# TensorE in recorded order, and memory given out by the recorder's clock, in a two-layer hybrid encoder trunk

## The chip, the core and the metric

The kernel runs on one core of one Trainium2 chip. The metric is the time of one execution on the device in microseconds; the median of several runs is taken. The engines are named as in the profile: PE is TensorE, DVE is VectorE, ACT is ScalarE, POOL is GpSimd, SP issues most DMAs.

## The reference

Two layers over a sequence of 256 tokens with 2048 channels. Each layer normalises, projects once to the columns of four token mixers and of four merge gates, runs the mixers, projects each mixer's output back, merges, and applies an output projection:

```
h = rms_norm(x, norm_g)
proj = h @ w_in                      # 13*512 + 256 + 4*2048 columns
A: ya = a_bg * conv3(a_cg * a_x) * silu(a_z)
B: yb = gqa_attention(rope(q), rope(k), v) * silu(b_z)
C: yc = rwkv7_bidir(h, c_r, c_k, c_v, ...) * silu(c_z)   # a scan in each direction
D: yd = silu(layer_norm(conv31(d_val * sigmoid(d_gate)) + dw_b)) * silu(d_z)
merged = sum_k sigmoid(gate_k + b_gate_k) * (y_k @ w_branch_k)
x = x + merged @ w_out
```

After both layers one more RMSNorm is applied. All is float32.

## The kernel before

Activations lie transposed: channels on the 128 partitions, the 256 tokens along the free axis. **The main stream** is the projections. Their weights arrive in 612 chunks of 128x1024 (`raw`), prefetched by DMA. `fetch` splits each chunk into two parts that TensorE takes at its fast rate: `hi`, a rounded copy made by ACT, and `lo`, the rest, made by DVE. `chunk` keeps three of them ahead. `wide` multiplies a chunk: for each of 8 blocks of 128 columns one `hi` matmul of 512 columns (x's own hi and lo side by side), and then for each block one `lo` matmul of 256 columns. `tile_b` makes one output tile of two chunks in a PSUM buffer `mg` (3 of them); `tile_branch` projects a mixer's output in the one buffer `mb`. After a tile `whole` adds its two halves: an ACT copy and a DVE addition, `arena<-mg`.

**The side work** is the four mixers: small float32 matmuls into four PSUM buffers `sd`, with ACT and DVE work between any two that hang together. In the trace and below, `bdS`, `bdT`, `bdE`, `bdM`, `bdR`, `bdX` and `rd` are constant buffers of mixer C, `part` is a two-part operand of A, B and C's norms. Mixer C's `rwkv` builds for each direction the inverses of small triangular blocks (`inverses`: two rounds of 32x32 products, `bdX` and then `bdT`, with an ACT copy each) and then goes through chunks of 64 tokens in sequence, two at a time (`chunks`). Mixer D's `conv_d` is 31 multiply-adds on DVE per 128 channels, all reading one input `u` and handed out three at a time; the tile `u` is given back at the end.

**Two things set the order.** First, the recorder: while `wide` and `passes` write down the projections, they call `pump` after each matmul, and `pump` steps the mixers, which are Python generators, where the kernel's own clock says that they are due. `now` is that clock's TensorE time; `clk` holds the times up to which DVE and ACT are taken; `due` is when the work of the step under way should be done. A step is next taken `SLACK` = 0.4 us after its `due`, and only while no engine of `clk` is further ahead of `now` than the side stream's `lead` (1.7 us and more). Second, the framework's scheduler goes over everything recorded after `first_x` and sets its own order on every engine, by priorities and its own estimates. Splits and prefetches are recorded at a high priority.

**The arena** is one SBUF tile from which the short-lived buffers of both streams come. `a` takes a piece (`Arena.get`), `f` gives it back (`Arena.put`) at recording time. Who gets the words next must wait on the engines for the last user. `get` prefers, among free stretches, those not given back within the last RECENT = 6 calls of `get` and `put`, then the tightest; pieces to keep (`keep`) come first-fit from the low end.

Of the kernel before, what the change touches and what calls it, by code (L numbers as in the profile page):

```python
# [21 lines left out]
DEPTH = 2  # L22
# [80 lines left out]
class Arena:  # L103


    U = 32
    RECENT = 6

    def __init__(self, ap, words):
        self.ap, self.n = ap, words // self.U  # L110
        self.when = np.zeros(self.n, np.int64)
        self.used = np.zeros(self.n, bool)
        self.live = {}
        self.tick = 0
        self.peak = 0

    def get(self, words, keep=False, take=True):

        m = -(-words // self.U)
        self.tick += 1  # L120
        best = None
        i = 0
        while i < self.n:
            if self.used[i]:
                i += 1
                continue
            e = i
            while e < self.n and not self.used[e]:
                e += 1
            if e - i >= m:  # L130

                j = i if keep else e - m
                key = i if keep else (int(self.when[j:e].max()) > self.tick - self.RECENT, e - i - m, -i)
                if best is None or key < best[0]:
                    best = (key, j)
            i = e
        if best is None:
            if not take:
                return False
            raise MemoryError(f"arena: {words} words asked, {(~self.used).sum() * self.U} free, live "  # L140
                              + str(sorted((v[1] * self.U, v[2]) for v in self.live.values())))
        j = best[1]
        if not take:
            return True
        self.used[j:j + m] = True
        self.peak = max(self.peak, int(self.used.sum()) * self.U * 4)
        return j, m
# [1 line left out]
    def free(self):  # L149
        return int((~self.used).sum()) * self.U  # L150

    def put(self, j, m):
        self.tick += 1
        self.used[j:j + m] = False
        self.when[j:j + m] = self.tick


class Side:
# [6 lines left out]
class Engine:  # L165
# [5 lines left out]
    def __getattr__(self, op):  # L171
        f = getattr(self.real, op)

        def call(out, *args, **kw):
            k = self.k
            if op == "preload_act_table_set":
                k.clk["scalar"] = max(k.clk["scalar"], k.now) + 1.3
                return f(out)  # L178
# [12 lines left out]
            else:  # L191
# [10 lines left out]
                else:  # L202
                    k.due = max(k.due, k.now) + cost
            return f(out, *args, **kw)  # L204

        return call
# [8 lines left out]
class Kern:  # L215
# [3 lines left out]
    RAW = 8  # L219
    BUSY = 0.7  # L220
    SLACK = 0.4
    LEAD = 1.7
    TWAIT = 24.0
    XSTEP = 1.0
# [30 lines left out]
    def a(self, shape, keep=False):  # L255
        words = int(np.prod(shape[1:]))
        if self.cur is None:

            t = self.now
            while not self.arena.get(words, keep, False) and self.now < t + 50:  # L260
                self.now += 0.2
                self.pump()
        j, m = self.arena.get(words, keep)
        if self.cur:
            self.cur.purse.net += m * Arena.U
        ap = self.arena.ap[:, j * Arena.U:j * Arena.U + words]
        if len(shape) > 2:
            names = "abcd"[:len(shape) - 1]
            ap = ap.rearrange(f"p ({' '.join(names)}) -> p {' '.join(names)}",
                              **{k: v for k, v in zip(names, shape[1:])})  # L270
        self.arena.live[id(ap)] = (ap, m, str(shape), j)
        return ap
# [9 lines left out]
    def f(self, *aps):  # L282
        for ap in aps:
            _, m, _, j = self.arena.live.pop(id(ap))
            self.arena.put(j, m)
            if self.cur:
                self.cur.purse.net -= m * Arena.U

# [24 lines left out]
    def add(self, gen, lead=None):  # L313

        e = Side(gen, self.now, lead or self.LEAD)
        if self.cur:
# [13 lines left out]
    def step(self, e):  # L330
# [9 lines left out]
        else:  # L340
            e.at = self.now + c if c > 0 else e.due + self.SLACK

# [386 lines left out]
    def conv_d(self, acc, i, u):  # L729
        nc = self.nc  # L730
        w = lambda j: self.pc("dw_w", j * NT + i)
        a = acc[:, i]
        nc.vector.tensor_scalar(a, u[:, 0:S], w(0), self.dwb2[:, i:i + 1], ALU.mult, ALU.add)
        for j in range(1, 31):
            nc.vector.scalar_tensor_tensor(a, u[:, j:j + S], w(j), a, ALU.mult, ALU.add)
            if j % 3 == 0:
                yield 0.9
        self.f(u)
# [48 lines left out]
    def rwkv(self, rkv, tl, cz):  # L787
# [5 lines left out]
        for d in range(2):  # L793
# [160 lines left out]
            for p in range(NT):  # L954
# [7 lines left out]
                for half in range(2):  # L962
# [9 lines left out]
                    def mm2(lhs, rhs, c0=0):  # L972
                        ps = self.pside()
                        for c in range(c0, 2):
                            a, b = cols[c]
                            self.blocks(ps[:, a:b], lhs(c), rhs[:, a:b], True, True)
                        return ps
# [165 lines left out]
    def layer(self, l):  # L1143
# [11 lines left out]
        for o, n, w, f in ((self.w0h, "w0", 8, 0.5), (self.a0h, "a0", 8, 0.5), (self.kah, "k_a", 4, 0.5),  # L1155
                           (self.dwb2, "dw_b", 4, 2.0), (self.gnb2, "gn_b", 4, 2.0)):
            nc.vector.tensor_scalar(o, par(n, w), f, None, ALU.mult)
# [179 lines left out]
    def run(self):  # L1337
        self.src = self.stream()
        self.ready, self.raws = [], []
        self.tiles = 0  # L1340
        self.consts()
        self.first_x()
        for l in range(DEPTH):
            self.layer(l)


@with_exitstack
# [5 lines left out]
def constants():  # L1353
# [4 lines left out]

    i = np.arange(P)
    put("ident", np.eye(P))  # L1360
    put("bdones", (i[:, None] // 64 == i[None, :] // 64) * 1.0)
    put("ones", np.ones((P, P)))

    perm = np.zeros((P, P))
# [105 lines left out]
```

## Time and profile before

| | us |
|---|---|
| median of 3 runs (1992.22 to 1999.15) | 1995.13 |
| the profiled execution | 1995.8 |
| its span on the core | 1993.9 |
| TensorE busy | 1934.8 |
| VectorE busy | 1439.8 |
| ScalarE busy | 1268.9 |

TensorE is busy through nearly all of the span. The rows that this text leans on stand in a section of their own below; a busy TensorE includes time in which its clock is granted at half, so both columns, busy and clock, have to be read.

### The profile page before, as it was taken

Reading aid. Unit: us, or ns where it says so; the run is one execution under the profiler, and the core shown is the slowest. Engines: PE = TensorE matmul, PEld = TensorE weight load, DVE = VectorE, ACT = ScalarE, POOL = GpSimd, SP = SyncE. Lnnn points to the kernel's source line nnn. Section 1 sums busy time; section 2 is a strip of 40 time slices with the busy share of each in tenths; the row PEclk is TensorE's granted clock in tenths of the full one; section 3 lists DMA queues with packets and bytes.
Section 4 is the critical chain, followed back from the end, with each engine's and each line's share of the span. In section 5 each row is a group of like instructions: output and inputs, shape, how many; then the busy total and the mean of one; then the engine's idle time right before and its main releaser. Section 6 shows DMA issues by size and latency. Waiting matters only on the chain.

```text
span 1993.9 us, 32440 instructions
## 1 busy us (share of the span) xinstructions
PE 1934.8 (97%) x12194; PEld 1716.7 (86%) x12194; DVE 1439.8 (72%) x2495; ACT 1268.9 (64%) x2293; POOL 71.6 (4%) x117
## 2 busy tenths in 40 slices
PE   8999999899999999999999999998999999999997
PEld 6888788799988898998888887888999989989986
DVE  7867858967787566666677778589787866566655
ACT  6776666567657766554567766766774577565454
POOL 1001010000101000000000010000001100000000
PEclk9999999899999999999999999999999999999998
DMA  7554443344655345566655554533555544456653
GB/s 247 186 181 165 159 156 117 117 165 166 197 181 180 137 150 179 202 206 205 214 186 185 181 169 143 154 114 138 177 171 187 195 143 159 155 184 207 203 190 136
DMA packets 97693, 343.19 MB, mean 172 GB/s; under 512 B 11808, under 2 KB 12192, under 8 KB 97536
## 3 DMA queue, kind: packets, MB, share of 16 engines
q1 hardware_dynamic: 93312, 331.48, 49.1%
q0 software_dynamic: 3648, 8.59, 1.7%
q8 instruction: 96, 1.57, 0.3%
q10 hardware_dynamic: 576, 1.05, 0.1%
q14 instruction: 61, 0.50, 0.1%
HBM read 332.48 MB, written 8.39 MB: 171 GB/s over the span
## 4 chain that ended last, share of the span: by engine, by line
PE 93%; ACT 3%; DVE 2%; DMA 1%; issue 1%; DVEq 0%; SPq 0%; POOL 0%; ACTq 0%; POOLq 0%
PE mg L204 74%; PE sd L204 9%; PE mb L204 9%; DVE arena L204 1%; DVE lo L204 1%; ACT arena L204 1%; ACT bdE L204 1%; DMA raw<-w 1%; ACT hi L204 1%; DMA scratch<-arena 0%; DMA arena<-xT 0%; ACT bdS L204 0%; ACT L178 0%; ACT bdT L204 0%; ACT bdR L204 0%
## 5 line engine op out<-in xcount | busy, mean ns | idle before, releaser
L204 PE MATMUL mg<-slab,hi 128*128 128x512 f32 x4368 | 1113.7, 396 | 17.1 <-DVE slab L204 9.5
L204 DVE TENSOR_TENSOR lo<-raw,hi 128x1024 fp32r<-128x1024 f32 x612 | 746.6, 1221 | 344.1 <-PE mg L204 247.2
L204 PEld LDWEIGHTS mg<-slab,hi 128*128 128x128 f32 x4368 | 789.6, 190 | 160.9 <-DVE slab L204 10.7
L204 ACT ACTIVATE hi<-raw 128x1024 fp32r<-128x1024 f32 x612 | 646.4, 1057 | 440.4 <-PE mg L204 294.7
L204 PE MATMUL mg<-slab,lo 128*128 128x256 f32 x4368 | 618.4, 285 | 1.7 <-DVE lo L204 1.5
L204 PEld LDWEIGHTS mg<-slab,lo 128*128 128x128 f32 x4368 | 585.9, 191 | 37.5 <-DVE lo L204 3.0
L204 DVE TENSOR_TENSOR arena<-arena 128x512 f32<-128x512 f32 (+16 forms) x389 | 166.1, 432 | 35.2 <-ACT arena L204 24.2
L204 DVE SCALAR_TENSOR_TENSOR arena<-arena,par 128x256 f32<-128x256 f32 x346 | 152.2, 479 | 7.8 <-ACT arena L204 6.7
L204 PE MATMUL mb<-slab,hi 128*128 128x256 f32 (+1 forms) x1040 | 156.8, 288 | 1.0 <-DVE slab L204 0.6
L204 PEld LDWEIGHTS mb<-slab,hi 128*128 128x128 f32 x1040 | 141.1, 192 | 5.7 <-DVE slab L204 0.8
L204 DVE TENSOR_TENSOR arena<-mg,arena 128x256 f32<-128x256 f32 x305 | 126.8, 418 | 18.0 <-ACT arena L204 15.3
L204 ACT ACTIVATE arena<-mg 128x256 f32<-128x256 f32 x241 | 89.7, 377 | 67.4 <-PE mg L204 52.3
L204 ACT ACTIVATE arena<-arena 128x256 f32<-128x256 f32 (+4 forms) x195 | 93.5, 497 | 29.5 <-DVE arena L204 26.1
L204 ACT ACTIVATE arena<-arena,b_gate 128x256 f32<-128x256 f32 x128 | 64.0, 503 | 54.9 <-DVE arena L204 54.4
L204 PE MATMUL mb<-slab,lo 128*128 128x256 f32 x528 | 87.2, 286 | 0.0
L178 ACT ACT_TABLE_LOAD x62 | 79.5, 1283 | 8.3 <-PE sd L204 5.0
L204 PEld LDWEIGHTS mb<-slab,lo 128*128 128x128 f32 x528 | 75.1, 192 | 1.6
L204 ACT ACTIVATE bdE<-sd 64x128 f32<-64x128 f32 x256 | 69.7, 272 | 7.5 <-PE sd L204 4.2
L204 DVE SCALAR_TENSOR_TENSOR slab<-arena,slab 128x512 fp32r<-128x512 f32 (+1 forms) x64 | 35.4, 555 | 34.8 <-ACT slab L204 34.7
L204 ACT ACTIVATE arena<-sd 128x64 f32<-128x64 f32 (+4 forms) x122 | 40.0, 332 | 17.3 <-PE sd L204 15.5
L204 DVE SCALAR_TENSOR_TENSOR arena<-arena 128x256 f32<-128x256 f32 (+1 forms) x80 | 37.1, 473 | 17.6 <-ACT arena L204 16.9
L204 PE MATMUL sd<-arena,bdE 128*128 128x128 f32 (+1 forms) x224 | 45.4, 285 | 3.9 <-ACT arena L204 3.3
(96 smaller groups left out, 1062.2 us busy)
## 6 DMA issues: line engine op xcount, KB each, us to landing
raw<-w SPq DMA_DIRECT2D x612, 512.0 KB, 3.3
arena<-xT SPq DMA_DIRECT2D x4, 512.0 KB, 8.3
scratch<-slab POOLq DMA_DIRECT2D x16, 128.0 KB, 2.7
scratch<-arena POOLq DMA_DIRECT2D x8, 256.0 KB, 4.2
arena<-xT SPq DMA_DIRECT2D x8, 256.0 KB, 3.8
x<-arena SPq DMA_DIRECT2D x8, 256.0 KB, 4.8
arena<-x SPq DMA_DIRECT2D x8, 256.0 KB, 3.6
arena<-lorab POOLq DMA_DIRECT2D x16, 96.0 KB, 2.9
```

The lines of the kernel that those rows point to most:

```text
L178: return f(out)
L204: return f(out, *args, **kw)
```

## The change

```diff
 class Arena:
     U = 32
-    RECENT = 6
...
-        self.when = np.zeros(self.n, np.int64)
+        self.when = np.zeros(self.n)
...
-    def get(self, words, keep=False, take=True):
+    def get(self, words, keep=False, take=True, now=0.0):
...
-                key = i if keep else (int(self.when[j:e].max()) > self.tick - self.RECENT, e - i - m, -i)
+                late = self.when[j:j + m].max() > now
+                key = (late, j) if keep else (late, e - i - m, -i)
...
-    def put(self, j, m):
-        self.tick += 1
+    def put(self, j, m, when):
         self.used[j:j + m] = False
-        self.when[j:j + m] = self.tick
+        self.when[j:j + m] = when
...
 class Kern:
     SLACK = 0.4
+    OVER = 1.5
...
-        j, m = self.arena.get(words, keep)
+        j, m = self.arena.get(words, keep, now=self.now)
...
-            self.arena.put(j, m)
+            self.arena.put(j, m, max(self.now, self.due, *self.clk.values()) + self.OVER)
...
-        for l in range(DEPTH):
-            self.layer(l)
+
+        with self.tc.manual_schedule(engines={mybir.EngineType.PE}):
+            for l in range(DEPTH):
+                self.layer(l)
```

In the two layers TensorE's instructions stay in the order in which they were recorded; ACT, DVE, POOL and SP are still ordered by the scheduler. A freed piece is stamped with the clock's latest time plus 1.5 us, and a request takes pieces whose stamp has passed by `now` before others. What is recorded is the same in both kernels: the same instructions in the same sequence (the numbers in the names differ by 2). In before TensorE's order steps back in the recorded sequence at 472 places, in after at one. The TensorE instructions that carry a wait go from 179 to 119, those of ACT from 839 to 749, those of DVE from 729 to 741.

**Place 1, DVE, mixer C's first direction in layer 0.** `arena<-sd_466,rd` makes the operand of the next `sd` matmul of the chunk sequence; the `par0` rows are `conv_d`, the `lo` rows are weight splits. Before:

```order
L204 SCALAR_TENSOR_TENSOR arena_69<-arena_69,par0_71 128x256 [waits DVE_49] x6
L204 TENSOR_TENSOR lo_524_3902<-raw_514_3842,hi_523_3901 128x1024 [waits DMAHW5_49,PE_49,Activation_49]
L204 SCALAR_TENSOR_TENSOR arena_69<-arena_69,par0_71 128x256 [waits DVE_49] x6
L204 TENSOR_TENSOR lo_529_3947<-raw_522_3899,hi_528_3946 128x1024 [waits DMAHW6_49,PE_49,Activation_49]
L204 TENSOR_TENSOR arena_69<-sd_466_3478,rd_105 128x64 [waits DVE_49]
L204 TENSOR_TENSOR arena_69<-sd_466_3478,consts_70 128x64
L204 SCALAR_TENSOR_TENSOR arena_69<-arena_69,par0_71 128x256 [waits DVE_49] x12
```

After:

```order
L202 TENSOR_TENSOR lo_461_3440<-raw_455_3404,hi_460_3439 128x1024 [waits DMAHW2_49,PE_49]
L202 TENSOR_SCALAR arena_69<-arena_69,par0_71,derived0_189 128x256 [waits DVE_49]
L202 SCALAR_TENSOR_TENSOR arena_69<-arena_69,par0_71 128x256 [waits DVE_49]
L202 TENSOR_TENSOR arena_69<-sd_466_3480,rd_105 128x64 [waits PE_49]
L202 TENSOR_TENSOR arena_69<-sd_466_3480,consts_70 128x64
L202 MEMSET arena_69 128x15 [waits DVE_49]
```

The operand stood behind runs of six `conv_d` rows and waited for DVE (for the last reader of its arena words, a `conv_d` row); now it stands some 30 rows earlier in DVE's queue, behind the split `lo_461` in place of `lo_529`, and waits for TensorE's product alone.

**Place 2, some 40 us further on, ACT, DVE and TensorE.** ACT's `arena<-sd_507` copies what the matmul `sd_512` takes (in before `sd_512` is `sd_512_3819` and reads the same copy). ACT before:

```order
L204 ACTIVATE arena_69<-mg_498_3732 128x256 [waits DVE_49]
L204 ACTIVATE arena_69<-mg_508_3804 128x256
L204 ACTIVATE arena_69<-sd_502_3751,arena_69 128x128 [waits PE_49]
L204 ACTIVATE arena_69<-sd_507_3790 128x256 [waits PE_49]
L204 ACTIVATE arena_69<-arena_69,b_gate0_188 128x256 [waits DVE_49] x2
```

ACT after:

```order
L202 ACTIVATE hi_510_3809<-raw_503_3767 128x1024 [waits DVE_49,DMAHW3_49,PE_49,Activation_49]
L202 ACTIVATE arena_69<-mg_498_3734 128x256 [waits DVE_49,PE_49]
L202 ACTIVATE hi_515_3846<-raw_509_3807 128x1024 [waits DVE_49,DMAHW4_49,PE_49,Activation_49]
L202 ACTIVATE arena_69<-arena_69,b_gate0_190 128x256 [waits DVE_49]
L202 ACTIVATE arena_69<-sd_507_3792 128x256 [waits DVE_49]
```

DVE after:

```order
L202 TENSOR_TENSOR lo_505_3770<-raw_499_3735,hi_504_3769 128x1024 [waits DMAHW2_49,PE_49,Activation_49]
L202 SCALAR_TENSOR_TENSOR arena_69<-arena_69,par0_71 128x256 [waits DVE_49]
L202 TENSOR_TENSOR arena_69<-mg_498_3734,arena_69 128x256 [waits Activation_49]
L202 SCALAR_TENSOR_TENSOR arena_69<-arena_69,par0_71 128x256 [waits DVE_49] x20
L202 TENSOR_TENSOR arena_69<-sd_512_3821,rd_105 128x64 [waits PE_49]
```

TensorE after (`sd_3792` is `sd_507`, `sd_3821` is `sd_512`):

```order
L202 MATMUL sd_3792<-bdE_83,bdT_77 128x128 x2
L202 MATMUL mg_3734<-slab_210,lo_3671 128x256 x4
L202 MATMUL mg_3806<-slab_207,hi_3737 128x512 x4
L202 MATMUL mg_3806<-slab_208,hi_3737 128x512 x4
L202 MATMUL sd_3821<-arena,bdE_83 128x128
```

The copy waited for its product alone; now it waits for DVE, and by the count in the built program that is the fifteenth of the twenty `conv_d` rows in one run, which stand behind the addition of tile `mg_498`. On TensorE four `lo` and eight `hi` matmuls lie between the product and the matmul that takes the copy. The same rows stand in layer 1 around `sd_1845`.

**Place 3, TensorE, the inverses of layer 0's second direction.** `sd_6191` (`sd_6193` after) is the `bdT` round of 32 products; ACT copies its result twice (32x512 each) before `sd_6227` (`sd_6229`) may start. Before:

```order
L204 MATMUL sd_6191<-bdT_77,arena 32x32
L204 MATMUL mg_6412<-slab_205,lo_6343 128x256 x2
L204 MATMUL sd_6191<-bdT_77,arena 32x32 x31
L204 MATMUL mg_6412<-slab_205,lo_6343 128x256 x2
L204 MATMUL mg_6412<-slab_206,lo_6343 128x256 x4
L204 MATMUL mg_6412<-slab_207,hi_6376 128x512 x4
L204 MATMUL mg_6412<-slab_208,hi_6376 128x512 x4
L204 MATMUL mg_6412<-slab_207,lo_6377 128x256 x4
L204 MATMUL mg_6412<-slab_208,lo_6377 128x256 x4
L204 MATMUL sd_6227<-bdE_83,bdT_77 128x128 x2
L204 MATMUL sd_6257<-arena,bdE_83 128x128
```

After:

```order
L202 MATMUL mg_6122<-slab_209,hi_6092 128x512 x4
L202 MATMUL mg_6122<-slab_210,hi_6092 128x512 x3
L202 MATMUL sd_6193<-bdT_77,arena 32x32 x32
L202 MATMUL mg_6122<-slab_210,hi_6092 128x512
L202 MATMUL sd_6229<-bdE_83,bdT_77 128x128 x2
L202 MATMUL mg_6122<-slab_209,lo_6093 128x256 x4
```

Twenty-two matmuls of projections recorded later lay between the two steps; now one `hi` matmul does. The same rows stand at four places, one for each direction and layer.

## Rows read from the trace of the kernel before

**Rows 1.** The page's head and busy times: engine, busy us (share of span), instructions.

```profile
span 1993.9 us, 32440 instructions
PE 1934.8 (97%) x12194; PEld 1716.7 (86%) x12194; DVE 1439.8 (72%) x2495; ACT 1268.9 (64%) x2293; POOL 71.6 (4%) x117
```

**Rows 2.** Busy times by stretch: start:end, length, busy (instructions) of each engine, clock, DMA.

```profile
200.00:250.00 50.00, 46.44 (x261) 38.70 (x261) 44.72 (x105) 31.76 (x60) 0.00 (x0) 1.00 0.47 158
...
300.00:350.00 50.00, 47.24 (x280) 42.48 (x281) 41.50 (x94) 33.28 (x86) 0.00 (x0) 0.93 0.36 121
350.00:400.00 50.00, 42.19 (x252) 37.51 (x251) 49.52 (x112) 28.91 (x64) 0.00 (x0) 0.90 0.32 112
...
700.00:1000.00 300.00, 300.00 (x1853) 269.91 (x1852) 189.35 (x259) 166.85 (x262) 0.00 (x0) 1.00 0.58 193
...
1350.00:1400.00 50.00, 46.14 (x290) 41.43 (x291) 48.59 (x103) 29.40 (x70) 0.00 (x0) 0.97 0.40 137
...
1981.00:1994.00 13.00, 0.04 (x1) 0.00 (x0) 5.83 (x6) 2.17 (x3) 3.43 (x2) 0.61 0.43 162
```

**Rows 3.** Chain of waits: start, length, what; its first and longest runs of matmuls.

```profile
9.46 20.28 PE mg L204 x96
...
908.92 88.83 PE mg L204 x507
```

**Rows 4.** TensorE's waits over the whole span: releaser, total us, times, longest.

```profile
PE sd L204 <- ACT bdS L204: 10.7, 8, 2.4
...
PE mg L204 <- DVE arena L204: 7.0, 4, 3.5
PE sd L204 <- ACT arena L204: 4.8, 10, 1.1
...
PE sd L204 <- ACT bdT L204: 2.2, 2, 1.3
```

**Rows 5.** Columns as in Rows 2, the six stretches at half clock.

```profile
1216.00:1222.70 6.70, 6.29 (x19) 5.13 (x19) 5.26 (x16) 1.44 (x2) 0.00 (x0) 0.50 0.10 39
...
sum 34.10, PE 31.59 PEld 28.17 DVE 27.02 ACT 12.87 POOL 0.00; mean PE 5.27 PEld 4.69 DVE 4.50 ACT 2.14 POOL 0.00
```

**Rows 6.** TensorE in order of time: start, length, operation, count, [idle before].

```profile
228.13 0.38 PE L204 MATMUL sd<-part,rounded 128*128 128x256 f32 x1 [0.66 <-ACT part L204]
229.82 0.39 PE L204 MATMUL sd<-part,rounded 128*128 128x256 f32 x1 [1.31 <-DVE part L204]
...
624.01 2.00 PE L204 MATMUL mg<-slab,hi 128*128 128x512 f32 x8
...
1352.20 3.61 PE L204 MATMUL mg<-slab,hi 128*128 128x512 f32 x8 [3.53 <-DVE arena L204]
```

**Rows 7.** TensorE and VectorE around 383, in order of time.

```profile
360.66 0.39 PE L204 MATMUL sd<-arena,bdE 128*128 128x128 f32 x2
...
383.20 0.77 PE L204 MATMUL sd<-arena 128*128 128x128 f32 x2 [2.66 <-DVE arena L204]
...
382.70 0.22 DVE L204 TENSOR_TENSOR arena<-sd,rd 128x64 f32<-128x64 f32 x1
...
382.97 4.83 DVE L204 SCALAR_TENSOR_TENSOR arena<-arena,par 128x256 f32<-128x256 f32 x12
```

**Rows 8.** Groups of instructions: operation, count, busy us, mean ns, idle before them.

```profile
L204 DVE TENSOR_TENSOR lo<-raw,hi 128x1024 fp32r<-128x1024 f32 x612 | 746.6, 1221 | 344.1 <-PE mg L204 247.2
...
L204 ACT ACTIVATE hi<-raw 128x1024 fp32r<-128x1024 f32 x612 | 646.4, 1057 | 440.4 <-PE mg L204 294.7
...
L204 DVE TENSOR_TENSOR arena<-mg,arena 128x256 f32<-128x256 f32 x305 | 126.8, 418 | 18.0 <-ACT arena L204 15.3 <-PE mg L204 2.2
L204 ACT ACTIVATE arena<-mg 128x256 f32<-128x256 f32 x241 | 89.7, 377 | 67.4 <-PE mg L204 52.3 <-DVE arena L204 9.0 <-DVE slab L204 2.6
...
L204 ACT ACTIVATE bdT<-sd 32x512 f32<-32x512 f32 x8 | 4.7, 589 | 1.5 <-PE sd L204 1.4
L204 ACT ACTIVATE arena<-sd 32x512 f32<-32x512 f32 x8 | 4.7, 582 | 0.1
```

More of the change, by code (lines that the diff above doesn't have):

```diff
@@ L106 @@
     U = 32
-    RECENT = 6
     def __init__(self, ap, words):
         self.ap, self.n = ap, words // self.U
-        self.when = np.zeros(self.n, np.int64)
+        self.when = np.zeros(self.n)
         self.used = np.zeros(self.n, bool)
         self.live = {}
-        self.tick = 0
         self.peak = 0
-    def get(self, words, keep=False, take=True):
+    def get(self, words, keep=False, take=True, now=0.0):
         m = -(-words // self.U)
-        self.tick += 1
         best = None
@@ L150, in free @@
         return int((~self.used).sum()) * self.U
-    def put(self, j, m):
-        self.tick += 1
+    def put(self, j, m, when):
         self.used[j:j + m] = False
-        self.when[j:j + m] = self.tick
+        self.when[j:j + m] = when
 class Side:
```

## The prediction

> **What bounds the kernel now.** I read the head of the page first: TensorE is busy 1934.8 of 1993.9 us, VectorE 72% and ScalarE 64% on the average [rows 1]. So TensorE sets the time, and only two things can be won: time in which it stands, and time in which it runs slowly. The table by stretch tells where both lie [rows 2]: 700 to 1000 is full at clock 1.00, while 200:250, 300:350, 350:400 and 1350:1400 fall short, and there TensorE waits inside mixer C's and D's work. In 350:400 VectorE is busy 49.52 of 50 us: that stretch has a second limit, to which I come back.
>
> Standing: 1993.9 − 1934.8 = 59.1 us. Of it 9.5 lie ahead of the first matmul [rows 3] and 13.0 behind the last [rows 2]; the change touches neither. **36.7 us** of waits are left inside. The waits by releaser say what they are [rows 4]: TensorE waiting for a side step's operand that ACT or DVE has not made (`bdS` 10.7, `arena` 7.0 and 4.8, and so on); weights hardly count.
>
> Slow running: six stretches with the clock at half (1.2 in place of 2.4 GHz), with 31.59 us of busy TensorE in them [rows 5]. Half of that would have done, so they cost **15.6 us**, 2.6 each. Eight `hi` matmuls take 3.61 us behind a gap of 3.53 us, and 2.00 us elsewhere [rows 6]. Each of the six follows a gap of 2.2 us or more (two of these gaps stand in [rows 6, 7]); the waits of 0.66 and 1.31 us at 228 [rows 6] lie in a stretch at 1.00 [rows 2].
>
> So 36.7 + 15.6 = 52.3 us is the ceiling of what an order can give, down to 1943.5 us from the profiled execution's 1995.8. That execution is 0.7 us above the median of 1995.13.
>
> **The change part by part.** No work is added or removed. The main stream's matmuls cost what they cost: 507 in 88.83 us where nothing disturbs [rows 3].
>
> *TensorE in recorded order: what goes.* In before the scheduler put projections recorded later ahead of side matmuls that were ready, and then let TensorE come to several side steps in sequence with nothing between. By before's order 33 side steps have under 1 us of TensorE work between what makes their operand and their use, and nearly all of the 36.7 us fell on those. In after such steps are 10 of 340. The waits of `bdS` (10.7) and of the `arena` operands [rows 4] are of this kind. I cost their removal at all of the 36.7, and the half clock behind them at all of the 15.6, and then add what the new order leaves.
>
> *Memory by the clock.* At 383 TensorE stood 2.66 us for an operand whose product had left TensorE at 360.66 + 0.39; DVE made it at 382.70, twenty us later [rows 7], because of the last reader of its arena words, a `conv_d` row, and of the queue behind which it stood (place 1 of the change). In after that wait is for TensorE alone. This is part of the sum above. The stamps themselves cost nothing: they are reckoned while the kernel is recorded.
>
> *New: the copy `arena<-sd_507` waits for `conv_d`* (place 2, once in each layer). Behind the end of tile `mg_498` come, one after the other: ACT's copy 0.38, DVE's addition 0.42 [rows 8], fifteen `conv_d` rows at 4.83/12 = 0.40 [rows 7], 6.0 together, and the copy itself, 0.38 as its like of the same size. That is 7.2 us; TensorE meanwhile has eight `hi` matmuls, 2.0 us [rows 6]. It stands 5.2 us. Lower end 4, since the run can't begin before the tile ends and only cheaper hand-offs could shorten it. Upper end 8.7, by adding the longest such wait of before, 3.5 [rows 4], for a VectorE that comes late to the run. In this stretch VectorE is busy 99% [rows 2], so I go above the plain sum and take 7. Two places: 14, and as gaps of that length were followed by half clock, 2 × 2.6 more: **19.2**. Queued behind the waiting copy on ACT are `bdS` copies and the next `hi` split, but those have a chunk or more in hand.
>
> *New: the inverses* (place 3, four times). ACT makes two copies, 0.58 + 0.59 [rows 8]; between stands one `hi` matmul, 2.00/8 = 0.25 [rows 6]. 0.9 us each: **3.7**. Ends 2 and 6 (a split of 1.06 us [rows 8] ahead of two of the copies). Before, this wait was 2.2 in all [rows 4], under 22 matmuls of cover.
>
> *The other tight steps.* By after's order 22 more side steps have under 1.6 us of TensorE work between, and 84 have 1.6 to 2.0. A step's own copy is 0.2 to 0.4 us, so they wait only where something stands ahead of it on ACT or DVE. Splits take 1.06 on ACT and 1.22 on DVE [rows 8], and 612 of each fill a third of either engine's time. A third of the 22 at 0.9, and a third of the 84 at 0.25, make 6.6 + 7 = 13.6; I take **13**. Ends: 3 (nearly all covered) and 28 (each of 26 steps as dear as one of before's 33, 36.7/33 = 1.1).
>
> *Weights.* In after each `lo` split has at least 3.75 us of TensorE work between what its queue needs and its first use, typically 4.6; each `hi` 6 or more. I cost it at nothing; DVE's stall at place 2 is its one danger, and that is the first rival.
>
> Left over: 19.2 + 3.7 + 13 = 36. Gain 52.3 − 36 = 16.3: 1995.8 − 16.3 = 1979.5, and 0.7 less against the median: **1979 us**. With the lower ends (2 × 6.6 + 2 + 3 = 18) 1961; with the upper ends (2 × 11.3 + 6 + 28 = 57, and three half-clock stretches more, 8) 2008.
>
> One rule speaks against the change. The trace first: TensorE's waits of about 1 us at 228 left the clock full [rows 2, 6]. The Trainium skill, "TensorE: Matmul & The Clock Gate", section "A second HAM failure mode: psum-queue depth-cycling", says that idling briefly and often between groups of matmuls can make the clock swing between its two levels. By that rule many short waits in place of few long ones would be dearer than their sum; the trace so far speaks against it.
>
> **The rivals.**
>
> *VectorE's shortage now holds TensorE (slower).* At 350:400 VectorE is full, and TensorE did only 42.19 × 0.90 = 38 us worth of work in 50; at 1350:1400, with VectorE at 48.59, 46.14 × 0.97 = 44.8 [rows 2]. Those 12 + 5.2 = 17.2 us I count as won. If `conv_d`'s work is what fills VectorE there, they stay, and a TensorE that may not take other projections first can't work round them. It decides when VectorE is behind by more than the 3.75 us that a `lo` split has in hand. Price: 17.2, with half clock behind four gaps, 10.4: 1979 + 27.6 = 2006 us. For it: the 99%. Against: the same work was there before, and at place 2 TensorE's stall of 7 us gives VectorE time to catch up.
>
> *The waits only trade places (no change).* The tight steps cost their upper end of 28 in place of 13: 1979 + 15 = 1994. For it: after has fewer very tight steps, but its middle step has 2.4 us between where before's had 4.4. Against: in before steps with 1.6 us and more hardly waited.
>
> *The memory waits don't bite, and tight steps are covered (much faster).* With VectorE early, or the run split up, only 3.7 + 6 are left: 1995.8 − 52.3 + 9.7 − 0.7 = 1952.5 us. Against it stands the built order itself.
>
> *Short waits lower the clock.* If ten of the tight steps were each followed by a half-clock stretch of 2.6: 26 more, 2005 us. It is the rule above taken at its word; the two waits at 228 are against it.
>
> **How the numbers follow.** Runs of this kernel lie within 0.2% of their median, so 0.3%, 6 us, is what a measurement can tell. My forecast 0.50, all of it faster; much faster 0.15; waits trade places 0.18; VectorE's shortage 0.12; the clock 0.05. Faster 0.65, same 0.18, slower 0.17. The range runs from 1953 (the much faster case, with half of its chance below) to 2004, which leaves out most of the two slower cases.
>
> **What would show it.** TensorE's waits for `bdS` near zero, where 10.7 stood; the gap at 383 gone; two gaps of 5 to 9 us, one in each layer, ahead of a matmul `sd<-arena,bdE`, with a long row of `conv_d` on VectorE beside it and half clock behind; four waits of about 1 us ahead of `sd<-bdE,bdT`; inner waits of about 30 us and two or three half-clock stretches in place of six. It would be wrong if waits for `lo` appear (VectorE's shortage), if the waits inside come to more than 45 us in many small ones (trade), or if the granted clock falls without a gap of 2 us before.

## The result and the profile after

The changed kernel takes 2026.16 us (2024.74 to 2028.87), against 1995.95 us of the kernel before beside it: a ratio of 1.0154, 95% interval 1.0132 to 1.0175. It is slower by some 30 us; the forecast was 1979 us, and the range ended at 2004.

The page's head of the kernel after, to be read against [rows 1]:

```profile
PE 1941.1 (96%) x12194; PEld 1710.8 (85%) x12194; DVE 1448.3 (72%) x2495; ACT 1267.8 (63%) x2293; POOL 71.0 (4%) x117
```

The span is 2023.8 us. TensorE is busy 6.3 us more and stands 2023.8 − 1941.1 = 82.7 us, against 59.1. Its waits by releaser over the span (total us, times, longest), against [rows 4]:

```profile
PE sd L202 <- ACT arena L202: 27.6, 16, 6.7
PE mg L202 <- DVE slab L202: 11.7, 5, 8.6
PE sd L202 <- DMA bdX<-scratch: 9.0, 2, 4.7
PE sd L202 <- DVE part L202: 7.3, 12, 1.3
PE sd L202 <- DVE arena L202: 5.3, 6, 1.8
PE sd L202 <- ACT bdT L202: 3.4, 4, 0.9
PE sd L202 <- ACT part L202: 3.1, 6, 0.7
PE sd L202 <- ACT bdS L202: 2.6, 7, 0.7
```

The 8.6 us ahead of the first matmul are within the second line. 61.4 us are left inside, against 36.7. What was to go has gone: `bdS` from 10.7 to 2.6, and no tile waits for `arena` any more (7.0). New are 27.6 for ACT's `arena` copies, 9.0 for a transfer, `bdX`, and some fifty short waits, the longest of them 2.18 us. Place 1's gap has gone too: no wait for DVE's `arena` is longer than 1.8.

By stretch (length, busy and instructions of PE, PEld, DVE, ACT and POOL, clock, DMA), against [rows 2] and two more stretches of before:

```profile
10.00:150.00 140.00, 140.00 (x789) 122.30 (x789) 110.64 (x183) 105.58 (x171) 5.79 (x9) 1.00 0.59 201
...
600.00:700.00 100.00, 97.14 (x736) 86.70 (x735) 64.16 (x113) 74.50 (x163) 5.04 (x8) 1.00 0.48 159
```

After:

```profile
10.00:150.00 140.00, 135.71 (x747) 116.42 (x747) 107.28 (x178) 102.89 (x166) 5.79 (x9) 0.99 0.57 190
...
200.00:250.00 50.00, 49.30 (x285) 40.80 (x283) 46.00 (x110) 31.77 (x59) 0.56 (x1) 1.00 0.49 160
...
300.00:350.00 50.00, 47.56 (x299) 41.94 (x298) 43.99 (x94) 37.09 (x88) 0.00 (x0) 1.00 0.42 137
350.00:400.00 50.00, 41.69 (x260) 37.35 (x260) 48.55 (x108) 26.68 (x64) 0.00 (x0) 0.93 0.35 111
...
600.00:650.00 50.00, 42.14 (x368) 36.79 (x367) 28.40 (x60) 34.31 (x79) 5.17 (x8) 0.93 0.42 126
...
1350.00:1400.00 50.00, 41.71 (x263) 37.43 (x263) 48.67 (x108) 26.81 (x65) 0.00 (x0) 0.93 0.34 112
```

TensorE is fuller than before in 200:250 (49.30 against 46.44) and somewhat in 300:350 (47.56 against 47.24, at clock 1.00 against 0.93). It is emptier where before was dense, in 10:150, and in 600:650 and 1350:1400 it stands for 8 us each. Two of the stretches at half clock and the sum of all, against [rows 5], and a wait in front of one of them:

```profile
382.20:389.00 6.80, 5.00 (x19) 4.61 (x20) 6.80 (x18) 0.38 (x1) 0.00 (x0) 0.50 0.00 0
...
662.10:665.50 3.40, 3.40 (x14) 3.00 (x13) 1.19 (x1) 1.69 (x3) 0.00 (x0) 0.50 0.02 6
...
sum 34.00, PE 27.37 PEld 24.53 DVE 21.80 ACT 8.70 POOL 0.00; mean PE 3.91 PEld 3.50 DVE 3.11 ACT 1.24 POOL 0.00
...
660.74 0.49 PE L202 MATMUL sd<-arena 128*128 128x128 f32 x2 [1.77 <-ACT arena L202]
```

They are seven now and add up to the same 34 us, with 27.37 us of busy TensorE in them. Half of that, 13.7 us, is what they cost, against 15.8 before (half of the 31.59 in [rows 5]). Hardly any gain came from there. Four of the seven stand at waits of 4.3 to 6.7 us. The other three, from 64.7, 662.1 and 1191.1 on, follow waits of 1.73, 1.77, and 0.64 and 1.24 us.

Three places carry the reading. First place 2 of the change (start, length, engine, operation, count, idle before):

```profile
375.33 2.00 PE L202 MATMUL mg<-slab,hi 128*128 128x512 f32 x8
384.00 0.79 PE L202 MATMUL sd<-arena,bdE 128*128 128x128 f32 x2 [6.67 <-ACT arena L202]
...
377.18 0.42 DVE L202 TENSOR_TENSOR arena<-mg,arena 128x256 f32<-128x256 f32 x1
377.52 8.00 DVE L202 SCALAR_TENSOR_TENSOR arena<-arena,par 128x256 f32<-128x256 f32 x20
...
383.57 0.38 ACT L202 ACTIVATE arena<-sd 128x256 f32<-128x256 f32 x1 [4.69 <-DVE arena L202]
```

The tile's addition ends at 377.6, the run of twenty `conv_d` rows follows, and the copy goes at 383.57, behind the fifteenth of them. TensorE stood 6.67 us, and again as long in layer 1.

Second, the inverses' transfer. POOL's queue and TensorE after:

```profile
608.82 2.63 POOL L202 DMA_DIRECT2D bdT<-scratch  x4 [2.33 <-DMA scratch<-arena]
611.58 1.29 POOL L202 DMA_DIRECT2D bdX<-scratch  x2
...
616.95 1.96 PEld L202 LDWEIGHTS sd<-bdX,slab 64*32 64x32 f32 x64 [4.93 <-DMA bdX<-scratch]
```

POOL loads `bdT` first and `bdX` behind it; the matmuls that need `bdX` are next in TensorE's order. Their weight load waits 4.93 us, TensorE stands 4.73. In before POOL had the same order:

```profile
605.13 2.63 POOL L204 DMA_DIRECT2D bdT<-scratch  x4 [2.16 <-DMA scratch<-arena]
608.64 1.29 POOL L204 DMA_DIRECT2D bdX<-scratch  x2 [0.87 <-issue]
...
619.03 1.20 PE L204 MATMUL sd<-bdX,slab 64*32 64x32 f32 x64
```

There TensorE came to those matmuls at 619.03, ten us behind the issue (in after 5.4), and had other work until then: the transfer was covered by the order.

Third, one of the many short waits (TensorE, then ACT):

```profile
313.99 0.38 PE L202 MATMUL sd<-arena,bdE 128*128 128x128 f32 x2
315.60 0.49 PE L202 MATMUL sd<-arena 128*128 128x128 f32 x2 [1.22 <-ACT arena L202]
...
312.48 2.26 ACT L202 ACTIVATE bdE<-sd 64x128 f32<-64x128 f32 x8
314.76 0.38 ACT L202 ACTIVATE arena<-mg 128x256 f32<-128x256 f32 x1
315.18 0.37 ACT L202 ACTIVATE arena<-sd,arena 128x128 f32<-128x128 f32 x1
```

The copy `arena<-sd,arena` takes 0.37 us, but stands on ACT behind eight `bdE` copies, 2.26 us in all, and a tile's copy. The matmul that takes it is next in TensorE's order, so TensorE stands 1.22 us.

### The profile page after: what moved, and what is told of

It reads as the page before. It is cut to its first block, busy times and chain, and to the rows that moved or that the text cites. A ratio compares the mean times of both kernels' runs of the same rounds, so it can differ in the third digit from the quotient of the medians.

```text
span 2023.8 us, 32281 instructions
## 1 busy us (share of the span) xinstructions
PE 1941.1 (96%) x12194; PEld 1710.8 (85%) x12194; DVE 1448.3 (72%) x2495; ACT 1267.8 (63%) x2293; POOL 71.0 (4%) x117
## 4 chain that ended last, share of the span: by engine, by line
PE 84%; DVE 6%; ACT 4%; issue 2%; DMA 2%; POOL 1%; DVEq 0%; SPq 0%; POOLq 0%; ACTq 0%
PE mg L202 67%; PE mb L202 9%; PE sd L202 8%; DVE arena L202 3%; DVE lo L202 2%; ACT bdE L202 1%; ACT arena L202 1%; DVE slab L202 1%; DMA bdX<-scratch 0%; ACT L176 0%; DMA arena<-scratch 0%; ACT hi L202 0%; DMA scratch<-arena 0%; DVE part L202 0%; DMA arena<-xT 0%
## 5 line engine op out<-in xcount | busy, mean ns | idle before, releaser
L202 PE MATMUL mg<-slab,hi 128*128 128x512 f32 x4368 | 1151.0, 399 | 11.7 <-DVE slab L202 11.7
L202 PEld LDWEIGHTS mg<-slab,lo 128*128 128x128 f32 x4368 | 603.9, 192 | 44.5 <-issue 2.7
L202 PE MATMUL mg<-slab,lo 128*128 128x256 f32 x4368 | 635.6, 286 | 0.0
L202 PE MATMUL mb<-slab,hi 128*128 128x256 f32 (+1 forms) x1040 | 150.2, 285 | 0.0
L202 PEld LDWEIGHTS mb<-slab,hi 128*128 128x128 f32 x1040 | 135.6, 192 | 0.6
L202 ACT ACTIVATE arena<-arena,b_gate 128x256 f32<-128x256 f32 x128 | 64.7, 505 | 78.8 <-DVE arena L202 78.5
L202 PE MATMUL sd<-arena 96*128 96x256 f32 (+3 forms) x224 | 44.6, 342 | 11.0 <-ACT arena L202 11.0
L202 PEld LDWEIGHTS sd<-arena,bdE 128*128 128x128 f32 x224 | 37.2, 191 | 20.1 <-ACT arena L202 14.2
L202 PE MATMUL sd<-arena,bdE 128*128 128x128 f32 (+1 forms) x224 | 39.9, 271 | 14.5 <-ACT arena L202 13.3
```

## The experiments

Two theories were set against each other at first: that the fixed order loses the time (TensorE now stands before every late step), or that the new memory does. Each part alone, then single causes, then parts of the order.

**The order alone.** The kernel before with the `manual_schedule` around the layers and its own arena.

```diff
-        for l in range(DEPTH):
-            self.layer(l)
+        with self.tc.manual_schedule(engines={mybir.EngineType.PE}):
+            for l in range(DEPTH):
+                self.layer(l)
```

> TensorE in recorded order, with the arena of the kernel before (RECENT). In the kernel after, TensorE stood 61.8 us between its first and last matmul, against 36.7 before; 13.7 of it are the two copies that wait for conv_d because of their memory, the rest are side steps that come late. Theory (the order loses it: TensorE now stands before each late step): about 2010 us, that is 2026 less the two copies and their half clock, with the waits for bdX of 9 us still there. Rival (the new memory loses it, the order wins): 1995 us or less.

Measured: 2032.55 us, ratio 1.0189 (1.0174 to 1.0204). The theory has the direction right and the size wrong, by 22 us: the order alone costs 38 us, more than the whole change, and beside it the new arena gives 6 us back. Its own costliest wait (the waits, then TensorE and VectorE in order of time, and last the same step in the kernel after):

```profile
PE sd L204 <- DVE arena L204: 31.6, 8, 8.7
...
606.83 1.19 PE L204 MATMUL sd<-arena,consts 128*128 128x256 f32 x2 [8.64 <-DVE arena L204]
...
605.53 1.15 DVE L204 TENSOR_TENSOR arena<-arena 128x512 f32<-128x512 f32 x2 [2.54 <-DMA scratch<-arena]
...
604.23 0.70 PE L202 MATMUL sd<-arena,consts 128*128 128x256 f32 x2 [1.81 <-DVE arena L202]
```

VectorE's sum for mixer D stands behind the last rows of the inverses in VectorE's queue, and then VectorE is idle for 2.54 us for a transfer that still reads the words: the old arena had given the sum memory of the inverses just written out. TensorE stands 8.64 us, in either layer; with the new arena the same step stands 1.81. But place 2 isn't the new arena's alone: here, too, TensorE stands 5.81 us in either layer (at 389.46 and 1392.89) for a result of VectorE behind a run of fourteen `conv_d` rows. Whether words or VectorE's order put it there, no run tells.

**The arena alone.** The new arena, TensorE scheduled.

```diff
-        with self.tc.manual_schedule(engines={mybir.EngineType.PE}):
-            for l in range(DEPTH):
-                self.layer(l)
+        for l in range(DEPTH):
+            self.layer(l)
```

> The new arena alone; TensorE ordered by the scheduler as before. Theory (the order loses it): 1990 to 2000 us, since the scheduler can put projections in front of late side steps. Rival (the memory loses it): 2010 us or more, with long waits of side steps for ACT arena copies that wait for conv_d.

Measured: 2016.10 us, ratio 1.0106 (1.0085 to 1.0128). The number is the rival's, but with the run before it both theories have a part: each change alone loses, and the new arena, which loses 22 us under the scheduler, wins 6 under the fixed order. The waits aren't the rival's either; the longest fall on tiles, not on side steps (ACT, then TensorE):

```profile
450.99 1.22 ACT L202 ACTIVATE arena<-mg 128x256 f32<-128x256 f32 x3
...
452.58 0.80 PE L202 MATMUL mg<-slab,hi 128*128 128x512 f32 x1 [3.92 <-DVE arena L202]
```

Three tiles' copies come in one row on ACT, and the next tile has no PSUM buffer for 3.92 us. It looked as though the stamps, made by the recorder's clock, were wrong for side steps which the scheduler puts back by tens of us. That was tried further down.

**The transfer: its step recorded later.** On the kernel after.

```diff
-    TWAIT = 24.0
+    TWAIT = 34.0
```

> The kernel after with TWAIT 34 in place of 24: the first step of the inverses is recorded 10 us of the recorder's clock later. In the kernel after TensorE stands 4.9 and 4.5 us for the transfer bdX in the second direction of each layer, with a half-clock stretch behind. Theory (a step recorded sooner than its operand lands, and TensorE can't go past it): these two waits are gone, about 2026 - 9.4 - 2 = 2014 us, unless the later chunks run into the end of the layer. Rival (TensorE would wait at the next late step instead): 2026 us, with the time found at other waits between 600 and 700 and between 1600 and 1700.

Measured: 2027.04 us, ratio 1.0166 (1.0150 to 1.0181), the same as after. The rival holds: no wait for `bdX` is left in the profile, but others took its place (of the waits):

```profile
PE sd L202 <- DVE arena L202: 11.7, 6, 4.8
```

Side steps wait 11.7 us for VectorE's `arena` results, where it was 5.3. The two longest, 4.79 us at 612.11 and at 1612.25, are the step of mixer D's sum from the first experiment, behind the inverses' rows on VectorE. Moving one chain by 10 us has made another step tight.

**The memory at place 2.** On the kernel after, `conv_d`'s input is stamped 12 us later.

```diff
-    def f(self, *aps):
+    def f(self, *aps, more=0.0):
...
-            self.arena.put(j, m, max(self.now, self.due, *self.clk.values()) + self.OVER)
+            self.arena.put(j, m, max(self.now, self.due, *self.clk.values()) + self.OVER + more)
...
-        self.f(u)
+        self.f(u, more=self.CONV)     # in conv_d; CONV = 12.0
```

> The kernel after, but the input tile of each conv_d is stamped 12 us later when it is given back, so that the copies of place 2 get other words and wait for their products alone. Theory (these are memory waits): the two waits of 6.8 us are gone, about 2026 - 13.7 - 2 x 1.5 = 2009 us. Rival (VectorE is short there, and the wait only moves to the next step that takes something from VectorE): 2020 us or more, with waits of several us between 350 and 400 and between 1350 and 1400 for VectorE.

Measured: 2008.94 us, ratio 1.0071 (1.0054 to 1.0087): 17 us less than after, as the theory says. The copy now goes as soon as its product is there, and TensorE doesn't stand (ACT, TensorE, and the stretch):

```profile
375.69 0.37 ACT L202 ACTIVATE arena<-sd 128x256 f32<-128x256 f32 x1
...
377.72 0.38 PE L202 MATMUL sd<-arena,bdE 128*128 128x128 f32 x2
...
350.00:400.00 50.00, 48.38 (x319) 43.65 (x318) 48.62 (x104) 30.46 (x72) 0.00 (x0) 1.00 0.44 142
```

VectorE is as full there as in after (48.62 of 50 us in 350:400, the last line), so the wait was memory, not VectorE's shortage.

**POOL's order.** As the last, with POOL in recorded order too, which puts `bdX` ahead of `bdT`.

```diff
-        with self.tc.manual_schedule(engines={mybir.EngineType.PE}):
+        with self.tc.manual_schedule(engines={mybir.EngineType.PE, mybir.EngineType.Pool}):
```

> As e4_conv_memory, with POOL in recorded order too. There the two loads of bdX are recorded ahead of the four of bdT, which take 2.6 us on POOL's queue and stood ahead of them. Theory (queue order on POOL is part of the wait for bdX): the two waits of about 4.8 us shrink by 2.6 each, about 2003 us. Rival (the scan on VectorE is late anyway and POOL's order hides behind it): 2009 us as e4_conv_memory.

Measured: 1994.39 us, ratio 0.9998 (0.9988 to 1.0008): 14.5 us less again, and level with the kernel before. That is below both figures expected. POOL's loads in e4_conv_memory, then POOL and TensorE here:

```profile
602.83 1.29 POOL L202 DMA_DIRECT2D bdX<-scratch  x2
...
598.87 1.34 POOL L202 DMA_DIRECT2D bdX<-scratch  x2 [3.07 <-DMA scratch<-arena]
600.20 2.71 POOL L202 DMA_DIRECT2D bdT<-scratch  x4
...
601.98 1.42 PE L202 MATMUL sd<-bdX,slab 64*32 64x32 f32 x64 [0.44 <-DMA bdX<-scratch]
```

The `bdX` wait is 0.44 us here, where it was 4.4 and 5.1. The loads go out 4 us sooner, more than the queue's 2.6, and the matmuls follow their issue by 3.1 us in place of 5.1 (they started at 607.93 there). The edit orders all that POOL does, so the 14.5 us aren't those of the two `bdX` loads alone: the waits for `bdX` fell by 8.4 us, those for `part` by 2.4, and the half clock costs 3.2 us less. This edit and the one before it give back 17.2 and 14.5 us, as much as the change had lost; the gain that was forecast is missing still. Against before, the waits inside are about as long (38.8 us by the same view), the half clock costs 6.8 us in place of 15.8, and TensorE is busy 8.4 us longer outside of it (see the last section).

**More reserve for each step.** As e4_conv_memory, with twice the slack.

```diff
-    SLACK = 0.4
+    SLACK = 0.8
```

> As e4_conv_memory, with SLACK 0.8 in place of 0.4: each side step is recorded 0.4 us later behind its due time. Theory (mixer C's chain of steps fills each layer, so reserve added to each step lengthens the layer): 2060 us or more, with TensorE standing before each merge of mixer C. Rival (the tight steps only lack a reserve, and 0.4 us each covers most of them): 1990 us or less.

Measured: 2117.66 us, ratio 1.0616 (1.0594 to 1.0637). The theory holds: mixer C's chain of steps is as long as the time that the projections give it. By stretch:

```profile
600.00:750.00 150.00, 150.00 (x927) 135.06 (x926) 121.80 (x209) 90.00 (x145) 7.21 (x12) 1.00 0.58 187
750.00:870.00 120.00, 80.73 (x501) 68.87 (x500) 34.93 (x87) 63.27 (x176) 4.43 (x7) 0.72 0.20 58
```

In 600:750 TensorE is full, then it does 80 of 120 us at a clock of 0.72 while the rest of the chain goes step by step ahead of mixer C's merges. Here a reserve couldn't be had by recording each step later.

**A fixed order in a part of the layer.** The kernel before, with its own arena; TensorE fixed from the 27th tile of a layer up to the first merge, scheduled elsewhere.

```diff
+    FIX = (26, 49)
...
+        fixed = ExitStack()
         for n, (kind, a, i) in enumerate(STREAM):
+            if n == self.FIX[0]:
+                fixed.enter_context(self.tc.manual_schedule(engines={mybir.EngineType.PE}))
+            if n == self.FIX[1]:
+                fixed.close()
```

> The kernel before (its own arena), but in each layer TensorE keeps the recorded order from the 27th to the 49th of the projection tiles, that is up to the first merge, and is scheduled elsewhere. Theory (the fixed order pays where the side steps' makers keep up with the recorder's clock, and loses where VectorE runs late, behind the first merge): the scheduler no longer piles up side steps in this stretch, whose waits cost before some 15 us a layer between 200 and 400; 1965 to 1985 us. Rival (a fixed order loses wherever it stands, since TensorE can't go past a late step): 2000 us or more.

Measured: 1972.23 us, ratio 0.9885 (0.9870 to 0.9900): faster than both kernels. By stretch, and of the waits:

```profile
10.00:150.00 140.00, 139.94 (x786) 122.11 (x787) 110.81 (x184) 105.48 (x171) 5.78 (x9) 1.00 0.60 200
...
350.00:400.00 50.00, 50.00 (x337) 45.94 (x336) 48.23 (x96) 31.64 (x70) 0.00 (x0) 1.00 0.49 159
```

```profile
PE sd L204 <- ACT bdS L204: 1.6, 3, 1.1
```

The theory holds. 10:150 stays as full as in before, 350:400 is full at clock 1.00, where [rows 2] has 42.19 at 0.90, and with VectorE at 48.23 of 50 us. `bdS` fell from 10.7 to 1.6. The waits inside are 24 us in place of 37, and the half clock costs 5 us in place of 16: so about half of the gain of 23 us is either's. Most of it shows in 300:400 and 1300:1400, at the end of the fixed part and just behind it (the first merge's matmuls start at 354.68 in layer 0).

**The complement.** Fixed from the first merge to the end of the loop over the tiles (`FIX = (49, 999)`). The layer's output projection stays scheduled, as do the first 26 tiles, so it and the run before don't add up to the whole layer.

> The complement: the kernel before with TensorE in recorded order from the first merge to the end of each layer, scheduled ahead of it. Theory (the loss lies there): 2020 us or more, with waits of several us for VectorE near 380, 600, 1380 and 1600. Rival (the loss is spread, a part in each stretch): 2000 to 2010 us.

Measured: 2038.97 us, ratio 1.0222 (1.0207 to 1.0237). The theory holds. Two of the stretches:

```profile
350.00:400.00 50.00, 36.22 (x207) 31.95 (x207) 48.07 (x112) 24.71 (x57) 0.00 (x0) 0.81 0.22 74
...
600.00:650.00 50.00, 40.51 (x358) 35.44 (x357) 31.64 (x64) 31.97 (x68) 5.07 (x8) 0.93 0.43 139
```

The two parts give −23 and +44 us, the order alone +38. That the scheduler here hands over side steps already put back, which the fixed order then has to take one by one, is a guess. But the sign of either part is plain. Whether the ends of such a block, inside a layer, also hold the scheduler back is not separated from the order itself by any run.

**Both together.** POOL fixed, the arena of e4_conv_memory, TensorE fixed in the 27th to the 49th tile.

```diff
+    FIX = (26, 49)               # as above
...
-        with self.tc.manual_schedule(engines={mybir.EngineType.PE}):
+        with self.tc.manual_schedule(engines={mybir.EngineType.Pool}):
```

> The new arena with conv_d's input stamped 12 us later and POOL in recorded order, as in e6_pool_order, but TensorE fixed only from the 27th to the 49th tile of each layer, as in h1_fixed_front. Theory (the fixed order is worth its gain ahead of the first merge, and there the new arena adds to it as e1 against the kernel after shows, 6 us): 1960 to 1972 us. Rival (the new arena hurts wherever the scheduler orders TensorE, as in e2_arena_only): 1980 us or more.

Measured: 1974.59 us, ratio 0.9896 (0.9880 to 0.9911). It is the same as h1_fixed_front and lies between the two figures expected: beside the fixed front the new arena and POOL's order add nothing, and they don't lose the 22 us of the arena alone either.

**Stamps that allow for the scheduler.** The arena alone, with a far later stamp.

```diff
-    OVER = 1.5
+    OVER = 45.0
```

> As e2_arena_only (new arena, TensorE scheduled), with OVER 45 in place of 1.5: a freed piece counts as ready only 45 us of the recorder's clock later, about as far as the scheduler put side steps back. Theory (the arena alone loses because its stamps don't know how far the scheduler puts a step back): 1995 us or less. Rival (the loss isn't the stamps; other words only shift the scheduler's order on ACT and DVE): 2005 us or more.

Measured: 1996.92 us, ratio 1.0016 (1.0001 to 1.0030). The 22 us of the arena alone are nearly gone, 2 us short of the figure expected. It speaks for the theory, but it is one value of one constant; that other words merely fell better isn't excluded.

## Why the prediction was wrong

**What bounds the kernel** was read rightly: TensorE, its waits inside (36.7) and its half clock (15.6, by the rows 15.8). **The waits that go** went (`bdS`, the tiles' `arena`).

**Place 2** was right: 7 us each forecast from [rows 7, 8], 6.67 measured, and half clock with it. The plain sum was 5.2; the tile's addition ended 1.5 us later than it assumed (377.6, not 375.33 + 0.38 + 0.42), so what I had added by judgement came out nearly right. Taking its cause away gave 17.2 us, against the 19.2 of the sum. **The inverses' `bdT` copies**: 3.7 forecast, 3.4 measured, four times 0.85.

**"The other tight steps", 13 us, is the first step that failed.** Measured: 61.4 − 2 × 6.7 − 9.0 − 3.4 = 35.6 us, beyond my upper end of 28. I had counted only weight splits as what may stand ahead of a copy on ACT or DVE. Counted in the trace, a split stands directly ahead of the late operand's maker in ten of the waits, a tile's copy or addition in five, and the side work's own rows in about half, as the eight `bdE` copies above; and in the fixed order TensorE does nothing else in that time. That half of the steps had under 2.4 us between, where before had 4.4, was before me; I gave it to a rival with 0.18.

**The transfer `bdX` had no term at all.** Its 9.0 us (e6_pool_order, which took them away with some others and the half clock behind, gave 14.5) stood in before's trace as a load issued at 608.64 whose matmuls came at 619.03. I had looked at `bdT`'s copies and their 22 matmuls of cover, not at the queue ahead of the step; POOL moves nothing in the change, and so I hadn't asked what its work had been hidden by.

**The half clock, all 15.6 us of it removed and 5.2 put back**, is the third: 13.7 us are there after. Place 2's share is 4.8, near the 5.2 forecast. 3.8 stand at the two `bdX` waits, which had no term, and 5.1 behind the three places with waits of 1.2 to 1.8 us. I had read from before that only gaps of 2.2 us and more are followed by it, and that isn't so.

The sum with these three: 1979.5 + 22.6 + 9.0 + 8.5 = 2019.6, less 0.9 for two terms and some 1.5 at the start and the end. The 8.4 us to the profiled execution's 2025.6 are in TensorE's busy time: outside of half clock it is 1941.1 − 13.7 = 1927.4 us, against 1934.8 − 15.8 = 1919.0, for the same matmuls. That they would take the same time was a fourth step that failed; its cause stays open.

**The rivals.** The slower one, VectorE's shortage, gave 2006 us and 0.12, but it isn't what happened: no wait for `lo` is in the profile, and h1_fixed_front shows TensorE full beside a VectorE that is 96% busy. The waits traded places, as the second rival had it, and two late copies and a late transfer came on top. The sign I named for it, more than 45 us of inner waits in many small ones, is what the profile shows: 61.4 us, 39 of them in waits of 2.18 us or less. The rival of the clock, to which I gave 0.05, had a small part: the sign I named for it, half clock without a gap of 2 us before, stands at three places, and costs 5 us in place of the 26 that I priced. Most short waits had no such sequel: 200:250 and 300:350 have several and stand at 1.00, and the wait of 2.18 us at 1012 left the clock full.

**What the change is worth** depends on where. The fixed order keeps the scheduler from piling up ready side steps, which is worth some 23 us in the tiles ahead of the merges; in the first 26 tiles it loses a little (135.71 of 140 us busy in 10:150). The scheduler's side matmuls ran far behind their recorded place: matched in the traces by name and number, 17, 28 and 35 us in the median of the three stretches of 50 us from 600 on, where after's stand at their place (within 0.6 us). That distance was the cover for the late transfer. But they ran as far behind ahead of the first merge, 15 to 22 us in 200:350, and there nothing is lost with it. So the distance alone doesn't part the two. As far as the runs tell, it is whether the makers are late, and behind the first merge they are: the `bdX` loads, `conv_d`'s run, the inverses' rows on VectorE. The fixed order gives the cover away, and `SLACK` didn't buy it back.

## What to carry to other kernels

Before an order is fixed, go through every step that the old order let slip, and look up in the trace when its operand really came, transfers and their queue included: a late producer that costs nothing under one order can be a wait under the other. Fix the order only where the producers keep up. And memory that is handed out by a planned time is as good as the plan is kept. A later stamp for the one buffer that a long run of queued work reads won 17 us here; it is one value, and no other was tried.

## What was not expected of the hardware

The same matmuls kept TensorE busy some 8 us longer in the fixed order, what half clock costs left out (1927.4 against 1919.0 us). It comes with the order and not with the arena: reckoned the same way, the order alone (e1_order_only) has 1925.7, e4_conv_memory 1927.1, e6_pool_order 1927.4, and h1_fixed_front, with the order fixed in a part, 1918.4. No run here tells why.

A wait's length alone didn't tell whether half clock followed. In after a wait of 2.18 us left the clock full, while waits of 1.73 and 1.77 us were followed by half clock, and so was a pair of 0.64 and 1.24.
